# Moving one spill pair and four accumulating transfers among the queues of a hybrid decoder layer

## The chip, the cores and the metric

The kernel runs on one core of a Trainium2 chip. The metric is the time of one execution on the device, in microseconds (us). A core has five engines that run side by side, each through its own list of instructions in order: TensorE (PE, matrix multiplies), VectorE (DVE), ScalarE (ACT), GpSimd (POOL) and SyncE (SP, which here only issues transfers). An engine whose next instruction waits for a semaphore holds up all that stands behind it in its list. Transfers (DMAs) are issued by SP, ACT or POOL and then run on 16 shared DMA engines.

## The reference

The kernel computes one layer of a decoder trunk for 512 positions and a width of 1024. What matters here is its first third:

```python
h = layer_norm(x, ln_emb_g, ln_emb_b)
proj = h @ w_in[i]
(q_att, c_kv, q_idx, k_idx, w_idx, cv_b, cv_c, cv_x, g_att, g_conv) = jnp.split(proj, split_points, axis=-1)
...
score = jnp.einsum('bqhs,bqh->bqs', jax.nn.relu(raw), wb.astype(jnp.float32))
_, sel = lax.top_k(score, topk)
...
conv_y = cv_b * causal_dwconv(cv_c * cv_x, mix_conv_w[i], mix_conv_b[i])
merged = (jax.nn.sigmoid(g_att + b_gate[i, 0]) * (att @ w_br_att[i])
          + jax.nn.sigmoid(g_conv + b_gate[i, 1]) * (conv_y @ w_br_conv[i]))
h = layer_norm(DEEPNORM_ALPHA * h + merged @ w_o[i], ln1_g[i], ln1_b[i])
```

A light indexer scores every earlier key, each query keeps its 128 best keys, and attention runs over those. A short gated convolution runs beside it. Both are gated, summed and projected, and the residual `ALPHA * h` is added. A gated MLP follows, which the change does not touch.

## The kernel before: how the work is staged

**Numbers.** All products are made in a reduced matrix format with a correction: each operand is split into a high and a low part, and three matmuls replace one (L157 to L159: high by high, low activation by high weight or the reverse). The weights come in chunks of 512 KB. A chunk goes through three stages: SP loads it (`wr`, L54), ACT makes the high part (`wh`, L76), and DVE or POOL makes the low part (`wl`, L143, by `Chunk.lo_eng`). Four raw buffers and four pairs of high and low parts rotate, so a load waits until the low part of the chunk four places before has been made.

**Steps.** `plan` writes the program as a list of steps, one chunk of matmuls each, and `run` (L1709) records them in order: first `advance` (loads and splits of chunks that are due), then the `preps` of that step in the order in which they were put there, then the step's own function. Every engine's list comes from this one recording. From step 5 on, `run` also takes some rounds of the top-k selection (`topk`, L588) behind every step. A round is a maximum of 8 and a replacement on DVE (L595, L597), 16 rounds make a block's selection, and a single DVE instruction turns it into a mask `madd` (L600). That is done for three blocks of queries, with 256, 384 and 512 keys.

The steps around the change are 0 to 3 (the indexer's queries `qi`), 4 and 5 (second halves of the first convolution inputs `c` and `x`, each followed by scores), 6 (convolution gate `b`; its number is `at_first`), 7 to 10 (attention queries `qa`), and 11 to 19 (three more triples `c`, `x`, `b` of the convolution). Steps 18 and 20 hold the first attention steps (`att_step`): PE makes logits, DVE and ACT make probabilities `p` (L670 to L678), and PE transposes them (`pT`, L686).

**Row sums.** The later gate products go by blocks (a 2 by 2 scheme in which sums of blocks of rows are multiplied). It needs four sums of the transposed activations `hx`, made in place by accumulating transfers that POOL issues (`first_sum`, L793 to L797). In the names of the order listing:

- sum 0: hx_282 += hx_404
- sum 1: hx_404 += hx_410
- sum 2: hx_410 += hx_282
- sum 3: hx_289 += hx_410

Each sum but the first writes a tile that the sum before it reads, or reads one that it writes, so a sum's issue waits until the sum before has landed. The results are split by `first_parts` at steps 15 to 19 and are first multiplied about 240 us into the run.

**Residual.** The residual `ALPHA * h` is prepared in DRAM. For each of the four blocks of x, DVE scales it by the gain (`res_gain`, L1027), SP spills it (`res_spill`, L1030, tensor `hsp`), and POOL issues a transfer that adds the scaled shift `be` onto it (`res_shift`, L1033). It is read back at about 284 us (`res_rows`). The scales of blocks 2 and 3 stand in `last_rows`, which step 5 calls between its matmuls and its scores (`self.between`, L934).

**Other POOL work there.** POOL also makes low parts of chunks (`wl`), the low part of a small weight (`w_uk`, `w_uv`, L623), the two additions of a convolution (`cvt`, L754), the low part of its result (`cvT`, L773) and of the attention queries (`qa`, L153).

The order is set by these lines of the kernel before:

```python
        for n in range(4):
            self.preps.setdefault((3, 5, 6, 7)[n], []).append(lambda n=n: first_sum(n))
...
        def last_rows():
            res_gain(2)
            res_gain(3)
...
                          (at_first, res_spill, 2), (at_first, res_spill, 3),
                          (at_first + 1, res_shift, 2), (at_first + 1, res_shift, 3), (at_slot[17], res_rows)):
```

Of the kernel before, what the change touches and what calls it, by code (L numbers as in the profile page):

```python
# [85 lines left out]
class Kern:  # L86
# [424 lines left out]
    def plan(self):  # L511
# [281 lines left out]
        def first_sum(n):  # L793

            b11, b12, b21, b22 = (self.hblock[g, h] for g in range(2) for h in range(2))
            to, what = ((b11, b12), (b12, b22), (b22, b11), (b21, b22))[n]
            nc.gpsimd.dma_start(to, what, accum_op=OP.add, max_dma_last_dim=4096)  # L797
# [168 lines left out]
        at_first = len(self.steps)  # L966
# [7 lines left out]
        at_slot, pairs = [], {}  # L974
        for i, o in enumerate(order):
# [24 lines left out]
            n = att_at.get(i)  # L1000
# [6 lines left out]

        self.preps.setdefault(2, []).append(first_flip)
        for n in range(4):
            self.preps.setdefault((3, 5, 6, 7)[n], []).append(lambda n=n: first_sum(n))  # L1010


        self.h1 = []
# [12 lines left out]
        def res_gain(b):  # L1026
            nc.vector.tensor_tensor(self.xb[b], self.xb[b], self.res["ge"], op=OP.mult)  # L1027

        def res_spill(b):
            nc.sync.dma_start(self.hdram[b], self.xb[b])  # L1030
# [16 lines left out]
        def last_rows():  # L1047
            res_gain(2)
            res_gain(3)

        self.between = last_rows
        for at, f, *v in ((1, res_scale, "ge"), (2, res_gain, 0), (2, res_gain, 1), (3, res_spill, 0), (3, res_spill, 1),
                          (1, res_load, "be", "ln_emb_b"), (4, res_scale, "be"), (5, res_shift, 0), (5, res_shift, 1),
                          (at_first, res_spill, 2), (at_first, res_spill, 3),
                          (at_first + 1, res_shift, 2), (at_first + 1, res_shift, 3), (at_slot[17], res_rows)):
            self.preps.setdefault(at, []).append(lambda f=f, v=v: f(*v))

        self.zps = {}
# [429 lines left out]
        n = len(those)  # L1488
# [323 lines left out]
```

## Time and profile before

| What | Value |
|---|---|
| Median of 3 runs | 747.59 us (747.19 to 749.47) |
| The profiled execution's own time | 747.88 us |
| Its span (first to last instruction of the program) | 746.1 us |
| Granted TensorE clock, mean | 0.988 |
| PE busy | 725.3 us (97%) |
| DVE busy | 615.0 us (82%) |
| ACT busy | 427.7 us (57%) |
| POOL busy | 264.5 us (35%) |
| DMA, mean | 244 GB/s |

The profile is one execution. Its views give, for every instruction, a start counted from the span's start, a duration, the idle time of its engine just before it and, in brackets, what ended that idle time. A row of a timeline merges neighbouring instructions of one line ("x2"), and then its duration runs from the first one's start to the last one's end. An instruction's recorded duration holds any time for which it was held up after its start. "SPq" marks an issue of a transfer by SP. POOL's issues of transfers occupy POOL itself.

### The profile page before, as it was taken

To read this page: it belongs to the slowest core of one execution; us is meant where nothing else is said; L and a number is where in the kernel's file an instruction comes from. 1 tells how busy PE (TensorE), PEld (TensorE's weight loads), DVE (VectorE), ACT (ScalarE), POOL (GpSimd) and SP (SyncE) were. 2 spreads that over 40 slices of the span, in tenths; PEclk is the share of its full clock that TensorE was granted. 3 is DMA by queue.
4 is the path that set the end of the run, shared out by engine and by line. 5 is a ranking of instruction groups with operands and counts; after the bars stand their busy time and mean duration, and the time that the engine had idled before them with its cause. 6 is when DMAs were issued, how large, how long until landed. Compare 5 with 4: busy or idle time off the path is not lost.

```text
span 746.1 us, 12222 instructions
## 1 busy us (share of the span) xinstructions
PE 725.3 (97%) x4399; PEld 639.9 (86%) x4399; DVE 615.0 (82%) x1041; ACT 427.7 (57%) x720; POOL 264.5 (35%) x336
## 2 busy tenths in 40 slices
PE   8999997979999999999999999999999999999995
PEld 5998885758887998888888999999999998888885
DVE  5878999977546765679898899999998899978796
ACT  5667322557776654442575666777777665655640
POOL 4315682757665860410101223433332212121002
PEclk9999999989999999999999999999999999999998
DMA  9468896777999999475997999989899869989761
GB/s 354 141 210 236 230 323 228 254 254 182 273 232 185 196 241 353 179 279 201 304 382 260 314 280 253 245 243 249 232 248 243 243 192 224 276 246 251 259 216 56
DMA packets 63019, 182.21 MB, mean 244 GB/s; under 512 B 7360, under 2 KB 7488, under 8 KB 62576
## 3 DMA queue, kind: packets, MB, share of 16 engines
q1 hardware_dynamic: 43968, 140.56, 53.8%
q0 software_dynamic: 18128, 39.46, 29.4%
q10 hardware_dynamic: 864, 1.43, 0.5%
q8 instruction: 34, 0.56, 0.3%
q14 instruction: 25, 0.20, 0.1%
HBM read 171.46 MB, written 72.88 MB: 327 GB/s over the span
## 4 chain that ended last, share of the span: by engine, by line
PE 83%; DVE 12%; DMA 2%; ACT 1%; issue 1%; SPq 0%; DVEq 0%; ACTq 0%
PE ffb L815 26%; PE gtb L815 5%; PE dn L1543 5%; PE dn L1542 5%; PE dn L1544 5%; DVE tk L597 4%; DVE m L595 3%; PE gt L157 2%; PE br L157 2%; PE wo L919 2%; PE wo L920 2%; PE br L159 2%; PE gt L159 2%; PE gt L158 2%; PE br L158 2%; PE wo L918 2%
## 5 line engine op out<-in xcount | busy, mean ns | idle before, releaser
L143 DVE TENSOR_TENSOR wl<-wr,wh 128x1024 fp32r<-128x1024 f32 (+1 forms) x175 | 198.1, 1148 | 42.3 <-ACT wh L76 41.6
L76 ACT CAST wh<-wr 128x1024 fp32r<-128x1024 f32 (+1 forms) x186 | 180.5, 978 | 76.1 <-DMA wr<-in_w_dn 13.5
L1469 POOL TENSOR_TENSOR behind<-token,neghalf 128x1 f32<-128x1 f32 x112 | 79.3, 815 | 242.1 <-ACT token L1468 205.7
L815 PE MATMUL ffb<-hsl,wh 128*128 128x256 f32 x304 | 86.0, 283 | 0.0
L815 PE MATMUL ffb<-hsh,wl 128*128 128x256 f32 x304 | 86.0, 283 | 0.0
L815 PE MATMUL ffb<-hsh,wh 128*128 128x256 f32 x304 | 86.0, 283 | 0.0
L815 PE MATMUL ffb<-h1T,wh 128*128 128x256 f32 x456 | 83.8, 283 | 0.0
L815 PEld LDWEIGHTS ffb<-h1T,wh 128*128 128x128 f32 x456 | 71.2, 192 | 0.1
L815 PE MATMUL ffb<-h1T,wl 128*128 128x256 f32 x228 | 64.7, 284 | 0.1
L815 PEld LDWEIGHTS ffb<-hsl,wh 128*128 128x128 f32 x304 | 58.4, 192 | 0.0
L815 PEld LDWEIGHTS ffb<-hsh,wh 128*128 128x128 f32 x304 | 58.4, 192 | 0.0
L815 PEld LDWEIGHTS ffb<-hsh,wl 128*128 128x128 f32 x304 | 58.4, 192 | 0.0
L143 POOL TENSOR_TENSOR wl<-wr,wh 128x1024 fp32r<-128x1024 f32 x15 | 39.8, 2711 | 18.0 <-ACT wh L76 18.0
L815 PEld LDWEIGHTS ffb<-h1T,wl 128*128 128x128 f32 x228 | 43.7, 192 | 0.4 <-DVE wl L143 0.3
L185 POOL TENSOR_TENSOR rstd<-veps,neghalf 128x1 f32<-128x1 f32 x12 | 8.0, 666 | 98.7 <-DVE nm L208 65.6
L1345 POOL DMA_DIRECT2D ws<-ws x38 | 37.5, 1084 | 13.4 <-issue 8.2
L1345 POOL DMA_DIRECT2D ws<-in_w_a x38 | 36.8, 1369 | 6.1 <-issue 2.7
L157 PE MATMUL cv<-hT,wh 128*128 128x512 f32 x80 | 32.4, 405 | 2.8 <-ACT wh L76 2.4
L159 PE MATMUL cv<-hT,wl 128*128 128x512 f32 x80 | 32.2, 402 | 2.3 <-POOL wl L143 2.3
L158 PE MATMUL cv<-hT,wh 128*128 128x512 f32 x80 | 31.9, 398 | 0.0
L742 DVE SCALAR_TENSOR_TENSOR ff<-c,vec,ff 128x510 f32<-128x510 f32 x38 | 28.5, 750 | 1.3
L739 ACT ACTIVATE ff<-c,vec 128x512 f32<-128x512 f32 x38 | 29.3, 812 | 0.5 <-DVE c L1390 0.5
(364 smaller groups left out, 2089.8 us busy)
## 6 DMA issues: line engine op xcount, KB each, us to landing
wr<-in_w_a SPq DMA_DIRECT2D x61, 512.0 KB, 4.5
ws<-in_w_a SPq DMA_DIRECT2D x76, 256.0 KB, 6.4
wr<-ws SPq DMA_DIRECT2D x38, 512.0 KB, 6.2
ws<-in_w_a POOLq DMA_DIRECT2D x38, 256.0 KB, 8.5
ws<-ws POOLq DMA_DIRECT2D x38, 256.0 KB, 10.9
wr<-in_w_b SPq DMA_DIRECT2D x15, 512.0 KB, 4.9
wr<-in_w_dn SPq DMA_DIRECT2D x15, 512.0 KB, 6.9
wr<-in_w_a SPq DMA_DIRECT2D x19, 256.0 KB, 6.7
```

The costliest lines, as they stand in the source:

```text
L76: nc.scalar.copy(hi, raw)
L143: (self.nc.vector if eng == "v" else self.nc.gpsimd).tensor_tensor(lo, raw, hi.bitcast(F32), op=OP.subtract)
L157: t.matmul(out, wh, xh, start=start, stop=False)
L158: t.matmul(out, wh, xl, start=False, stop=False)
L159: t.matmul(out, wl, xh, start=False, stop=stop)
L597: nc.vector.match_replace(nxt, m8, cur, PICKED)
L815: nc.tensor.matmul(o, l[:, c], r, start=start and c + i == 0, stop=stop and c == 3 and i == 2, skip_group_check=True)
L1345: return lambda: nc.gpsimd.dma_start(to, what, accum_op=OP.add, max_dma_last_dim=4096)
L1469: nc.gpsimd.tensor_tensor(self.sm("behind", [P, 1], bufs=2), t, self.neghalf, op=OP.mult)
L1542: nc.tensor.matmul(o, ah, wh[:, i, c], start=first, stop=False, skip_group_check=free)
L1543: nc.tensor.matmul(o, ah, wl[:, i, c], start=False, stop=False, skip_group_check=free)
L1544: nc.tensor.matmul(o, al, wh[:, i, c], start=False, stop=last, skip_group_check=free)
```

## The change

Three edits, none of which adds or removes an instruction:

1. Row sums 0 to 3 are issued at steps 3, 4, 5, 6 and no longer at 3, 5, 6, 7.
2. The spills of blocks 2 and 3 stand in `last_rows`, behind the two scales, and no longer at step 6.
3. The shifts of blocks 2 and 3 are issued at step 6, behind row sum 3, and no longer at step 7.

```diff
         for n in range(4):
-            self.preps.setdefault((3, 5, 6, 7)[n], []).append(lambda n=n: first_sum(n))
+            self.preps.setdefault(3 + n, []).append(lambda n=n: first_sum(n))
...
         def last_rows():
             res_gain(2)
             res_gain(3)
+            res_spill(2)
+            res_spill(3)
...
-                          (at_first, res_spill, 2), (at_first, res_spill, 3),
-                          (at_first + 1, res_shift, 2), (at_first + 1, res_shift, 3), (at_slot[17], res_rows)):
+                          (at_first, res_shift, 2), (at_first, res_shift, 3),
+                          (at_slot[17], res_rows)):
```

What this makes of the engines' lists is seen in two places. The first is POOL's list from row sum 1 on. `hx` rows are row sums, `hsp` rows are shifts (180 to 183 are blocks 0 to 3), and the numbers behind the names tell tiles apart. Before:

```order
L797 DMA hx_404<-hx_410 128x1024
L1033 DMA hsp_180<-be 128x1024
L1033 DMA hsp_181<-be 128x1024
L623 TENSOR_TENSOR w_uk<-w_uk_raw,w_uk 128x512
L754 TENSOR_TENSOR cvt_956<-cvt_956,tap_958 128x511
L754 TENSOR_TENSOR cvt_956<-cvt_956,tap_961 128x510
L143 TENSOR_TENSOR wl_1023<-wr_608,wh_1022 128x1024
L797 DMA hx_410<-hx_282 128x1024
L773 TENSOR_TENSOR cvT_1062<-cvy_1060,cvT_1062 128x512
L143 TENSOR_TENSOR wl_1078<-wr_766,wh_1077 128x1024
L797 DMA hx_289<-hx_410 128x1024
L1033 DMA hsp_182<-be 128x1024
```

The same stretch of POOL's list with the change:

```order
L797 DMA hx_404<-hx_410 128x1024
L797 DMA hx_410<-hx_282 128x1024
L1033 DMA hsp_180<-be 128x1024
L1033 DMA hsp_181<-be 128x1024
L623 TENSOR_TENSOR w_uk<-w_uk_raw,w_uk 128x512
L754 TENSOR_TENSOR cvt_957<-cvt_957,tap_959 128x511
L754 TENSOR_TENSOR cvt_957<-cvt_957,tap_962 128x510
L143 TENSOR_TENSOR wl_1026<-wr_608,wh_1025 128x1024
L797 DMA hx_289<-hx_410 128x1024
L1033 DMA hsp_182<-be 128x1024
L1033 DMA hsp_183<-be 128x1024
L773 TENSOR_TENSOR cvT_1065<-cvy_1063,cvT_1065 128x512
```

Row sum 2 now stands right behind row sum 1, ahead of the shifts of blocks 0 and 1 and of `w_uk`. Row sum 3 and the shifts of blocks 2 and 3 now stand ahead of `cvT` and the low part behind it, and no longer behind them. What follows on POOL (`qa`, `wl`, `w_uv` and so on) keeps its order.

The second place is SP's list, from the third chunk load before the spills on. `wr` rows are chunk loads, `hsp` rows are spills, and the first `ws` row begins a series of copies of weights for a later stage. Before:

```order
L54 DMA wr_845<-in_w_a 128x1024
L54 DMA wr_920<-in_w_a 128x1024
L54 DMA wr_1026<-in_w_a 128x1024
L1030 DMA hsp_182<-x_73 128x1024
L1030 DMA hsp_183<-x_74 128x1024
L1333 DMA ws_116<-in_w_a 128x512
```

And with the change:

```order
L54 DMA wr_845<-in_w_a 128x1024
L54 DMA wr_921<-in_w_a 128x1024
L1030 DMA hsp_182<-x_73 128x1024
L1030 DMA hsp_183<-x_74 128x1024
L54 DMA wr_1029<-in_w_a 128x1024
L1335 DMA ws_116<-in_w_a 128x512
```

The two spills have passed one chunk load (its tile is called wr_1026 before and wr_1029 after). PE, DVE and ACT execute the same instructions in the same order as before.

## The prediction

> **What bounds the kernel now.** I read the page first, then PE's idle times, then the chain of work that ended last, and then the timelines of POOL and DVE in the stretch that the change touches. The shares of that chain by engine, from the page:
>
> ```profile
> PE 83%; DVE 12%; DMA 2%; ACT 1%; issue 1%; SPq 0%; DVEq 0%; ACTq 0%
> ```
>
> PE is the bound but not all of it: 12% of the chain is DVE. So the question is where PE stands still for DVE. The timeline of PE, its rows with idle time between 90 and 170 us (start, duration, instruction, in brackets the idle time before it and what ended it):
>
> ```profile
> 94.96 0.50 PE L159 MATMUL cv<-hT,wl 128*128 128x512 f32 x1 [0.21 <-POOL wl L143]
> 127.16 0.79 PE L157 MATMUL cv<-hT,wh 128*128 128x512 f32 x1 [2.43 <-ACT wh L76]
> 130.44 0.80 PE L159 MATMUL cv<-hT,wl 128*128 128x512 f32 x1 [2.06 <-POOL wl L143]
> 147.31 0.50 PE L157 MATMUL cv<-hT,wh 128*128 128x512 f32 x1 [0.37 <-DVE cvy L770]
> 162.11 0.45 PE L686 MATMUL pT<-ident,p 128*128 128x128 f32 x1 [3.62 <-DVE p L678]
> 164.99 0.45 PE L686 MATMUL pT<-ident,p 128*128 128x128 f32 x1 [1.79 <-DVE p L678]
> ```
>
> These six sum to 10.48 us, and they are what any speed-up of the other engines here can give back. The last two wait for DVE's probabilities. The chain of work that ended last shows what made DVE late:
>
> ```profile
> 95.92 13.52 DVE madd L600
> ...
> 161.67 3.18 DVE p L678 x5
> ```
>
> One DVE instruction, the mask of the first selection, lasts from 95.92 to 109.44. The waits at 127.16 and 130.44 hang on it too: ACT and POOL, in their order, stood behind a convolution input that DVE made only after it. POOL's timeline over the same time:
>
> ```profile
> 84.94 1.29 POOL L773 TENSOR_TENSOR cvT<-cvy,cvT 128x512 fp32r<-128x512 f32 x1 [6.64 <-ACT cvT L772]
> 86.19 2.40 POOL L143 TENSOR_TENSOR wl<-wr,wh 128x1024 fp32r<-128x1024 f32 x1
> 88.54 0.89 POOL L797 DMA_DIRECT2D hx<-hx  x1
> 89.13 2.10 POOL L1033 DMA_DIRECT2D hsp<-be  x2
> 90.25 2.30 POOL L153 TENSOR_TENSOR qa<-qac,qa 128x512 fp32r<-128x512 f32 x1
> 91.51 3.40 POOL L143 TENSOR_TENSOR wl<-wr,wh 128x1024 fp32r<-128x1024 f32 x1
> ...
> 102.33 2.25 POOL L153 TENSOR_TENSOR qa<-qac,qa 128x512 fp32r<-128x512 f32 x1
> 103.58 5.70 POOL L143 TENSOR_TENSOR wl<-wr,wh 128x1024 fp32r<-128x1024 f32 x2
> ```
>
> POOL runs without a pause from 84.94 to 109.28, and the mask ends 0.16 us later. I read this as DVE kept out of something that POOL holds. Ahead of the three issues a POOL instruction starts when the one before it ends (86.19 against 84.94 + 1.29 = 86.23). Behind them it starts 1 us early: `qa` at 90.25 while the second shift's issue runs to 91.23, `wl` at 91.51 while `qa` is recorded to 92.55. From the issues on POOL always has its next instruction begun, and there is no seam for DVE.
>
> Where POOL runs without that overlap, DVE does get in at a seam. A later mask on DVE's timeline, and POOL's:
>
> ```profile
> 130.73 1.11 DVE L600 TENSOR_SCALAR madd<-tk 128x384 f32<-128x384 f32 x1
> ```
>
> ```profile
> 130.34 1.29 POOL L773 TENSOR_TENSOR cvT<-cvy,cvT 128x512 fp32r<-128x512 f32 x1
> 131.58 2.51 POOL L143 TENSOR_TENSOR wl<-wr,wh 128x1024 fp32r<-128x1024 f32 x1
> ```
>
> This mask ended at 131.84, 0.21 us after `cvT` (130.34 + 1.29 = 131.63), with POOL's next instruction standing right behind. The same at 170 us, DVE and then POOL:
>
> ```profile
> 169.31 2.12 DVE L143 TENSOR_TENSOR wl<-wr,wh 128x1024 fp32r<-128x1024 f32 x1
> ```
>
> ```profile
> 167.62 2.71 POOL L754 TENSOR_TENSOR cvt<-cvt,tap 128x511 f32<-128x511 f32 x2 [2.87 <-ACT tap L753]
> 170.30 3.40 POOL L143 TENSOR_TENSOR fsl<-hx,fsh 128x1024 fp32r<-128x1024 f32 x1
> ```
>
> DVE ended 1.09 us after the pair at 170.33, and POOL's next lasted 3.40 where a free one takes 2.40 (86.19 row).
>
> **The change part by part.** Row sum 2 moves ahead of the shifts of blocks 0 and 1 and of `w_uk`. POOL's timeline there now, and the time from issue to landing of the four row sums:
>
> ```profile
> 62.07 0.88 POOL L797 DMA_DIRECT2D hx<-hx  x1
> 62.67 2.06 POOL L1033 DMA_DIRECT2D hsp<-be  x2
> 69.99 1.91 POOL L623 TENSOR_TENSOR w_uk<-w_uk_raw,w_uk 128x512 fp32r<-128x512 f32 x1 [5.25 <-ACT w_uk L622]
> 71.88 2.78 POOL L754 TENSOR_TENSOR cvt<-cvt,tap 128x511 f32<-128x511 f32 x2
> 75.08 2.38 POOL L143 TENSOR_TENSOR wl<-wr,wh 128x1024 fp32r<-128x1024 f32 x1 [0.42 <-ACT wh L76]
> 77.40 0.89 POOL L797 DMA_DIRECT2D hx<-hx  x1
> ```
>
> ```profile
> DMA to landing us min/median/max: 5.9/7.0/7.7
> ```
>
> Row sum 2 waits at the head of POOL's list for row sum 1 (62.07) to land: at 69.1 by the median, 68.0 to 69.8 by the ends. Three issues take 2.66 us (62.07 to 64.73), so POOL is free at 71.7. Then `w_uk` at 1.29 (the size of `cvT`) and the pair at 2.78 end at 75.8, and `wl` starts 0.7 us later than 75.08. With another tenth for DVE's scores, which take turns with these three, I take 0.8 (0 to 1.5 by the landings; a gain is excluded, since `wl` waits for ACT until 75.08). Queued behind the waiting issue are just these; POOL idles there today until 69.99.
>
> DVE's scores and the first rounds move along by 0.8, and with them `cvy`, on which `cvT` waits by way of ACT (the 84.94 row). DVE's timeline:
>
> ```profile
> 72.31 7.28 DVE L585 SCALAR_TENSOR_TENSOR score<-rl,widx,score 128x512 f32<-128x512 f32 x6 [1.56 <-ACT rl L583]
> ...
> 83.51 0.68 DVE L770 TENSOR_TENSOR cvy<-cv,cvt 128x512 f32<-128x512 f32 x1
> ```
>
> So POOL's long run starts at 85.74. Row sum 3 and the shifts of blocks 2 and 3 leave that run: they took it from 88.59 to 91.23, 2.64 us. They now go into the pause between 78.3 and 85.7, if nothing holds them. Row sum 3 waits for row sum 2 (issued at 69.1, landed by 76.8 at the latest row). The shifts wait for the spills. DVE's scales, SP's issues, and the landing of the two spills now:
>
> ```profile
> 68.39 2.35 DVE L1027 TENSOR_TENSOR x<-x,ge 128x1024 f32<-128x1024 f32 x2
> ```
>
> ```profile
> 62.14 15.68 SPq L54 DMA_DIRECT2D wr<-in_w_a  x3
> 77.91 1.13 SPq L1030 DMA_DIRECT2D hsp<-x  x2
> ```
>
> ```profile
> DMA to landing us min/median/max: 7.5/8.1/8.7
> ```
>
> SP issues the spills at 77.91 because they stand behind a chunk load that waits for a raw buffer. In front of it they go at the scales' end, the second at 70.74, and land at 79.4 by today's 8.7. The traffic beside them is heavier (row sum 2 and two shifts), so I allow up to 83. The last issue then ends between 80.9 and 84, ahead of 85.74. The load that they pass goes out when POOL's `wl` is done, as before, and costs nothing.
>
> Now the run: `cvT` 85.74, `wl` to 89.4, `qa` to 90.7, `wl` to 93.1, `w_uv` to 94.4, `qa` to 95.7, `wl` to 98.0 (1.29 and 2.38 each). The mask comes at 96.7 and enters at the seam at 98.0; with the 0.21 us of the later mask it ends at 98.25, 11.2 us earlier than 109.44.
>
> [...]
>
> What is late next? With 11.2 us, `p` is there at 150.9 while PE, rid of 0.21, 2.43, 2.06, 0.37 and 3.62, comes for it at 153.4. The second batch (164.99) would be there at 153.8, PE at 154.5. POOL's `wl` for the 130.44 wait is done 11 us earlier as well. So all 10.48 us go. Against it, the 0.8 us of lateness can show as a wait for the next `wl`, as at 94.96: between 0 and 0.8, I take 0.3, the size of that row. The sum is -10.48 + 0.3 = -10.2 us.
>
> The profiled execution took 747.88 us (span 746.1, so 1.8 lie around it), 0.3 above the median of 747.59. 747.88 - 10.2 = **737.7 us**. Less would go where a shifted DVE instruction meets another POOL one, 2.4 us each at most, of which PE's slack of 2.5 us hides the most; so 736.5 to 741 for this case.
>
> **The rivals.** *The run stays closed.* The overlap could come from the chain of ready POOL instructions itself and not from the issues ahead of it. Then the mask ends when the run does: 109.44 - 2.64 + 0.8 = 107.6, 1.8 us earlier, and PE gains that: 746.0. A hole could open ahead of the last `wl`, whose high part waits for a load:
>
> ```profile
> 104.90 1.05 ACT L76 CAST wh<-wr 128x1024 fp32r<-128x1024 f32 x1 [3.97 <-DMA wr<-in_w_a]
> ```
>
> That gives 105.95 against a POOL that is there at 105.4 (98.0 and two `qa` and two `wl` more); the mask would enter then and end at 105.6, a gain of 3.8: 744.1. For this rival: 13.52 us is the only row of its length. Against it: two seams did let DVE in. I take 745, the middle.
>
> *The spills land late (slower).* POOL sits on the last shift, and `cvT` with the whole run behind it. The run without issues lasts 109.28 - 84.94 - 2.64 = 21.7 us, the last issue about 1 us. A landing after 84 puts the issues in front of the run again and the mask waits through; it ends as late as now for a landing at 86.7, and each us after that costs one. The spill at 70.74 would have to take 16 us, against 8.7 in the row. At twice that row, 88.1, the time is 749.3, and the `wl` that PE then needs is late as well: 749 to 751. [...]
>
> *Nothing changes.* A landing between 84 and 86.7, or a mask that gains and then loses it to other POOL instructions: 746 to 748.
>
> **How the numbers follow.** Main case 0.66, closed run 0.18, late spills 0.08, nothing 0.08. About 0.3% (2.2 us, so below 745.3) is what a measurement of this kernel can tell. The main case is faster, and the closed run half of it: 0.66 + 0.09 = 0.75. Same: 0.09 + 0.08 = 0.17. Slower: 0.08. The range takes the main case from 736.3 and the closed run to 746.2, and leaves out the other two and some edges.
>
> **What would show it.** Right: the first mask lasts about 1.5 us or less; POOL's row sum 3 and two shifts lie before 85 us; PE's waits at 127, 130 and 162 are gone. Wrong: the first mask still ends with POOL's run, or `cvT` on POOL waits behind a shift, or PE's waits return elsewhere by 170 us.

## The result, and the profile after

The changed kernel took 736.57 us (median; 735.2 to 737.32), the kernel before, run beside it, 748.4 us (747.19 to 749.47). The ratio is 0.984, with a 95% interval of 0.9816 to 0.9864: 1.6% faster. The forecast was 737.7 us, in a range of 736.3 to 746.2. The profiled execution took 735.2 us with a span of 733.4, against 747.88 and 746.1 before: 12.7 us less. The ratios in this document leave out executions in a slower state of the chip, one of them here: 746.65 us, of the kernel with the spills' part alone.

The chain's shares by engine, from the page of the kernel after:

```profile
PE 81%; DVE 13%; DMA 3%; issue 1%; ACT 1%; SPq 0%; DVEq 0%; ACTq 0%
```

They hardly differ from before (83% and 12%). The shares of a chain do not show a stall of 13 us in 746; the waits do. PE's timeline of the kernel after, the same stretch as before, all rows with an idle time of 0.2 us or more and the first gate matmul behind them:

```profile
89.89 0.50 PE L159 MATMUL qa<-hT,wl 128*128 128x512 f32 x1 [0.52 <-POOL wl L143]
...
153.28 0.82 PE L686 MATMUL pT<-ident,p 128*128 128x128 f32 x4 [1.53 <-DVE p L678]
...
155.66 0.50 PE L157 MATMUL gt<-hT,wh 128*128 128x512 f32 x1
```

The waits at 94.96, 127, 130, 147 and 162 are gone. The last of the six is left, at 153.28, and one at 89.89 is new: 2.05 us together. The first gate matmul of the kernel before, on the same view:

```profile
168.50 0.50 PE L157 MATMUL gt<-hT,wh 128*128 128x512 f32 x1
```

From 168.50 to 155.66 is 12.84 us, so the whole gain is made by this point. DVE's timeline of the kernel after, the first mask and one of the eight scalings of the probabilities:

```profile
97.16 0.46 DVE L600 TENSOR_SCALAR madd<-tk 128x256 f32<-128x256 f32 x1
...
150.75 2.39 DVE L678 TENSOR_SCALAR p<-p,rs 128x128 f32<-128x128 f32 x1
```

The mask lasts 0.46 us instead of 13.52 and ends at 97.62, 11.8 us earlier. The scaling comes beside a `wl` of POOL's (150.71, 2.35 us) and ends 0.08 us after it; the first scalings take 0.28 us each. That is not new, as the same scaling of the kernel before shows:

```profile
162.46 2.38 DVE L678 TENSOR_SCALAR p<-p,rs 128x128 f32<-128x128 f32 x1
```

POOL's timeline of the kernel after:

```profile
69.21 0.85 POOL L797 DMA_DIRECT2D hx<-hx  x1 [6.19 <-DMA hx<-hx]
...
78.67 0.89 POOL L797 DMA_DIRECT2D hx<-hx  x1
79.26 1.19 POOL L1033 DMA_DIRECT2D hsp<-be  x1
80.95 0.86 POOL L1033 DMA_DIRECT2D hsp<-be  x1 [0.50 <-issue]
86.18 1.30 POOL L773 TENSOR_TENSOR cvT<-cvy,cvT 128x512 fp32r<-128x512 f32 x1 [4.37 <-ACT cvT L772]
...
91.06 2.39 POOL L143 TENSOR_TENSOR wl<-wr,wh 128x1024 fp32r<-128x1024 f32 x1
94.91 1.30 POOL L623 TENSOR_TENSOR w_uv<-w_uv_raw,w_uv 128x512 fp32r<-128x512 f32 x1 [1.47 <-ACT w_uv L622]
96.17 1.29 POOL L153 TENSOR_TENSOR qa<-qac,qa 128x512 fp32r<-128x512 f32 x1
97.43 2.46 POOL L143 TENSOR_TENSOR wl<-wr,wh 128x1024 fp32r<-128x1024 f32 x1
```

The transfers are out of the run, as predicted. The mask (97.16 to 97.62) got in at the seam between `qa` and `wl` (97.43 to 97.46). But there is a row that the prediction did not have: POOL now **pauses** for 1.47 us ahead of `w_uv`. ScalarE's timeline of the kernel after says why, the load's issue and the high part that waits for it:

```profile
85.75 0.34 ACTq L620 DMA_DIRECT2D w_uv_raw<-in_w_uv  x1
...
94.21 0.62 ACT L622 CAST w_uv<-w_uv_raw 128x512 fp32r<-128x512 f32 x1 [5.25 <-DMA w_uv_raw<-in_w_uv]
```

The same two rows of the kernel before:

```profile
84.50 0.33 ACTq L620 DMA_DIRECT2D w_uv_raw<-in_w_uv  x1
...
90.54 0.62 ACT L622 CAST w_uv<-w_uv_raw 128x512 fp32r<-128x512 f32 x1 [2.83 <-DMA w_uv_raw<-in_w_uv]
```

Before, the load came 6.0 us after its issue, and POOL, kept busy by three transfers to issue, came for it later. Now it takes 8.4 us, and POOL is there first. The shifts' transfers, issued at 79.26 and 80.95, run beside it: the load took 6.4 us in the kernel with the row sums alone (below), whose shifts are issued behind it, and 8.2 in the one with the spills and shifts alone. So two things changed at once ahead of the mask: no transfer is issued in the run, and the run has a pause in it. The experiments have to tell which one lets DVE in.

### The profile page after: what moved, and what is told of

It reads as the page before. It is cut to its first block, busy times and chain, and to the rows that moved or that the text cites. A ratio compares the mean times of both kernels' runs of the same rounds, so it can differ in the third digit from the quotient of the medians.

```text
span 733.4 us, 12223 instructions
## 1 busy us (share of the span) xinstructions
PE 721.4 (98%) x4399; PEld 638.0 (87%) x4399; DVE 604.3 (82%) x1041; ACT 427.3 (58%) x720; POOL 268.4 (37%) x336
## 4 chain that ended last, share of the span: by engine, by line
PE 81%; DVE 13%; DMA 3%; issue 1%; ACT 1%; SPq 0%; DVEq 0%; ACTq 0%
PE ffb L815 22%; PE gtb L815 5%; PE dn L1546 5%; PE dn L1545 5%; PE dn L1544 5%; DVE tk L597 4%; DVE m L595 3%; PE gt L157 2%; PE br L157 2%; PE gt L159 2%; PE wo L919 2%; PE wo L920 2%; PE br L158 2%; PE gt L158 2%; PE br L159 2%; PE wo L918 2%
## 5 line engine op out<-in xcount | busy, mean ns | idle before, releaser
L1471 POOL TENSOR_TENSOR behind<-token,neghalf 128x1 f32<-128x1 f32 x112 | 85.3, 871 | 239.0 <-ACT token L1470 204.3
L1347 POOL DMA_DIRECT2D ws<-ws x38 | 39.9, 1200 | 11.4 <-issue 6.1
L143 POOL TENSOR_TENSOR wl<-wr,wh 128x1024 fp32r<-128x1024 f32 x15 | 36.3, 2421 | 17.7 <-ACT wh L76 17.7
L157 PE MATMUL cv<-hT,wh 128*128 128x512 f32 x80 | 31.4, 392 | 0.0
L158 PE MATMUL cv<-hT,wh 128*128 128x512 f32 x80 | 31.1, 389 | 0.0
L1273 ACT ACTIVATE ff<-ff 128x512 f32<-128x512 f32 x22 | 13.8, 633 | 27.2 <-DVE ff L742 27.2
```

Of the source, the lines that this page charges most:

```text
L143: (self.nc.vector if eng == "v" else self.nc.gpsimd).tensor_tensor(lo, raw, hi.bitcast(F32), op=OP.subtract)
L157: t.matmul(out, wh, xh, start=start, stop=False)
L158: t.matmul(out, wh, xl, start=False, stop=False)
L1347: return lambda: nc.gpsimd.dma_start(to, what, accum_op=OP.add, max_dma_last_dim=4096)
L1471: nc.gpsimd.tensor_tensor(self.sm("behind", [P, 1], bufs=2), t, self.neghalf, op=OP.mult)
```

## The experiments

Kernels that are set side by side ran on the same chip with the kernel before, four at a time in the order of the table (medians of the kernel before 749.32, 748.51 and 749.65 us). The "seam theory" in the expectations of the first group is the prediction's: transfers make POOL's records overlap, which leaves no seam. Theory A is the form that the first group left of it: a transfer that POOL issues at the head of an unbroken run keeps DVE out until POOL next pauses. Theory B arose from the first group: no transfer matters as such, and DVE gets in only where POOL's next instruction has become ready late. Theory C is on PE's clock.

| kernel | first mask us | median us | ratio to before, 95% interval |
|---|---|---|---|
| after + one POOL transfer behind `w_uv` | 13.01 | 750.04 | 0.9989 to 1.0016 |
| after + two of them | 13.63 | 752.81 | 1.0026 to 1.0056 |
| before, masks with an accumulator | 0.42 | 733.02 | 0.9767 to 0.9797 |
| row sums alone | 12.60 | 750.59 | 1.0008 to 1.0041 |
| after + a POOL subtraction behind `w_uv` | 1.11 | 738.17 | 0.9836 to 0.9887 |
| after, `w_uv`'s load earlier | 0.73 | 737.13 | 0.9827 to 0.9892 |
| before, two mask instructions with accumulators | 0.42 | 736.20 | 0.9812 to 0.9863 |
| before + PE kept busy in its waits | 13.51 | 747.12 | 0.9964 to 0.9996 |
| after + POOL transfer ahead of `w_uv` | 0.56 | 735.64 | 0.9779 to 0.9857 |
| after + the transfer from ScalarE | 1.42 | 736.99 | 0.9796 to 0.9876 |
| spills and shifts alone | 0.30 | 734.73 | 0.9748 to 0.9860 |
| after, masks and p with accumulators | 0.42 | 739.01 | 0.9818 to 0.9894 |

### One transfer put back

```diff
+        junk = [self.dram.tile([P, R], F32, name=f"junk{i}", tag=f"junk{i}") for i in range(1)]
+        for t in junk:
+            self.preps[8].append(lambda t=t: nc.gpsimd.dma_start(t, self.kvg))
```

> The changed kernel with one small extra transfer (64 KB, from a loaded constant to a scratch tensor that nobody reads) issued by POOL between w_uv and the second qa, in the middle of the run in which the first mask comes. Seam theory (an issue of a transfer right ahead of ready POOL instructions makes them overlap, and DVE finds no seam until POOL stands still): the first mask, 0.46 us in the changed kernel, lasts 11 to 13 us and ends when the run does, at about 110; the time goes back to 746 to 749. It is open whether one issue, which is 0.3 us longer than the time to the next start, is enough. Rival (the mask came free because transfers moved out of this time, or because of POOL's pause at 93.4 to 94.9): both are still so, the issue costs its own 0.9 us on POOL, the mask lasts at most 3 us, 736 to 738.

Measured: 750.04 us (748.52 to 750.82), as slow as the kernel before. One transfer of 64 KB that nobody waits for gives the whole 13 us back. DVE's timeline, then POOL's:

```profile
97.17 13.01 DVE L600 TENSOR_SCALAR madd<-tk 128x256 f32<-128x256 f32 x1
```

```profile
94.96 1.29 POOL L623 TENSOR_TENSOR w_uv<-w_uv_raw,w_uv 128x512 fp32r<-128x512 f32 x1 [1.52 <-ACT w_uv L622]
96.19 0.61 POOL L1684 DMA_DIRECT2D junk<-kvg  x1
96.82 1.31 POOL L153 TENSOR_TENSOR qa<-qac,qa 128x512 fp32r<-128x512 f32 x1
98.07 2.42 POOL L143 TENSOR_TENSOR wl<-wr,wh 128x1024 fp32r<-128x1024 f32 x1
...
105.30 4.73 POOL L143 TENSOR_TENSOR wl<-wr,wh 128x1024 fp32r<-128x1024 f32 x2
```

Everything up to 96 us is as in the kernel after, DVE comes to the mask at the same moment, and it ends with POOL's run again (110.18 against 110.03). One sign of the prediction falls: behind the transfer `wl` starts at 98.07, only 0.06 us ahead of the end of `qa` (96.82 + 1.31 = 98.13), so the 1 us overlap of POOL's records is not needed for the run to be closed. The transfer itself is over long before; the DMA view of this kernel, its last column the median time from issue to landing:

```profile
junk<-kvg POOLq DMA_DIRECT2D x1, 64.0 KB, 5.0
```

Issued at 96.19, it had landed by about 101.2, and DVE stayed out for 9 us more.

### Two transfers put back

The same line with `range(2)`.

> The same with two such small transfers in a row. Seam theory: the overlap is 0.6 us or more, the mask waits for the end of the run, 747 to 750. Rival: 1.8 us on POOL, 736 to 739. If the kernel with one issue is fast and this one slow, the overlap has to reach a size before it closes the seams.

Measured: 752.81 us and a mask of 13.63 us. The second transfer adds its own length to the run (0.55 us) and closes nothing more. The median is 2.8 us above that with one transfer, and the profile, of the fastest of the five executions (750.38 us), does not show where the rest comes from.

### The mask in a form that does not wait

```diff
-            nc.vector.tensor_scalar(self.madd[b], cur, LIMIT, DROP, op0=OP.is_ge, op1=OP.mult)
+            nc.vector.tensor_scalar(self.madd[b], cur, LIMIT, DROP, op0=OP.is_ge, op1=OP.mult,
+                                    accum_out=self.sm("mark", [P, 1], bufs=2))
```

> The kernel before, whose only change is that the three mask instructions also write out an accumulated value that nobody reads. All transfers and issues stand where they stood. Seam theory (the mask waits for something that POOL's instructions hold, and this form does not need it): the first mask lasts under 1 us although POOL runs overlapped from 90 to 109 as before, and the time falls by most of what the change gave: 735 to 739. Rival (the time came from where the transfers stand): nothing moves, 746 to 749. If this form needs the same thing, 746 to 749 too, with a mask of 13 us; then only the profile tells.

Written so, the kernel does not compute the layer (relative error 0.87): I take it to leave out the mask's multiplication by `DROP` (-1e30), so that the other keys stay in, and only its time counts. Measured: 733.02 us (732.49 to 733.71), the fastest of all. DVE's timeline, then POOL's:

```profile
95.87 0.42 DVE L600 TENSOR_SCALAR_CACHE_REDUCE madd<-tk 128x256 f32<-128x256 f32 x1
```

```profile
93.83 2.27 POOL L624 TENSOR_TENSOR w_uv<-w_uv_raw,w_uv 128x512 fp32r<-128x512 f32 x1
95.09 2.27 POOL L153 TENSOR_TENSOR qa<-qac,qa 128x512 fp32r<-128x512 f32 x1
```

This is the kernel before with its transfers in the run, POOL's closed run is just where it was (`w_uv` at 93.83 against 93.88, `qa` at 95.09 against 95.11), and the mask takes 0.42 us in the middle of it. So the 13.52 us were a wait beside POOL's run that this form (0.42 us) does not have, and the gain hangs on the masks alone; the other two, which have the new form as well, had lasted 1.11 and 0.43 us.

### Row sums alone

```diff
-            self.preps.setdefault((3, 5, 6, 7)[n], []).append(lambda n=n: first_sum(n))
+            self.preps.setdefault(3 + n, []).append(lambda n=n: first_sum(n))
```

> The first edit alone: row sums at steps 3 to 6, spills and shifts where they were. Two issues (the shifts of blocks 2 and 3) still stand in front of the run. Seam theory: the overlap stays, the mask lasts over 10 us, 746 to 749 (the run is 0.6 us shorter by one issue and starts 1.2 us later), unless POOL pauses for w_uv before the mask comes, which would open the seams. Rival (the row sums' place is what counts): 736 to 740.

Measured: 750.59 us, ratio 1.0008 to 1.0041, so if anything slower than before. DVE's timeline, then POOL's:

```profile
97.30 12.60 DVE L600 TENSOR_SCALAR madd<-tk 128x256 f32<-128x256 f32 x1
```

```profile
89.91 1.75 POOL L1033 DMA_DIRECT2D hsp<-be  x2
...
94.69 1.91 POOL L623 TENSOR_TENSOR w_uv<-w_uv_raw,w_uv 128x512 fp32r<-128x512 f32 x1
95.95 1.90 POOL L153 TENSOR_TENSOR qa<-qac,qa 128x512 fp32r<-128x512 f32 x1
```

Two shifts still stand in the run, POOL has no idle time behind them, and the run is closed. The records overlap by 0.65 us here (94.69 + 1.91 = 96.60 against 95.95), by 1 us before and by 0.06 us in the run above, with a mask of 12.6 to 13.5 us in all three.

### A subtraction in place of the transfer

```diff
+        fill = self.small.tile([P, 256], F32, name="fill", tag="fill", bufs=1)
+        done = self.small.tile([P, 256], F32, name="done", tag="done", bufs=1)
+        nc.gpsimd.memset(fill, 0.0)
+        self.preps[8].append(lambda: nc.gpsimd.tensor_tensor(done, fill, fill, op=OP.subtract))
```

> The kernel after, with one more subtraction on POOL (256 elements of a scratch tile, about 0.65 us by half of cvT's 1.30) put between w_uv's low part and the second qa, where the first of the junk transfers stood; no transfer is added. Theory A (a transfer issued ahead of POOL's run is what shuts VectorE out): nothing is issued there, so the first mask gets in at an early seam, under 3 us, and the time is that of the kernel after plus at most 0.6, 736 to 738. Theory B (VectorE gets in only at a seam where POOL's next instruction had become ready late, under about a us before the running one ended): POOL is 0.65 us later, ScalarE's high part for the next wl is ready 1.3 us before the seam, the seam stays shut as with the junk transfer: first mask 12 to 13.5 us, time 748 to 751.

Measured: 738.17 us, a mask of 1.11 us. DVE's timeline, then POOL's:

```profile
97.28 1.11 DVE L600 TENSOR_SCALAR madd<-tk 128x256 f32<-128x256 f32 x1
```

```profile
96.37 0.61 POOL L1685 TENSOR_TENSOR done<-fill 128x256 f32<-128x256 f32 x1
96.94 1.30 POOL L153 TENSOR_TENSOR qa<-qac,qa 128x512 fp32r<-128x512 f32 x1
98.20 2.47 POOL L143 TENSOR_TENSOR wl<-wr,wh 128x1024 fp32r<-128x1024 f32 x1
```

The subtraction takes 0.61 us in the place where the transfer took 0.61 us, POOL's next instructions come within 0.13 us of where they came there, and the mask gets in at the seam at 98.20. Theory B falls: POOL's order and lateness are the same in both kernels, and only the kind of the instruction differs. ScalarE's high part for the `wl` at the seam was ready 1.33 us ahead of it there and 1.28 us here. This pair is the cleanest of the study.

### The load of w_uv one step earlier

```diff
+        def latent_load(name):
+            self.latent_w[name] = self.k2(f"{name}_raw")
+            nc.scalar.dma_start(self.latent_w[name], a[name])
...
+        self.preps.setdefault(7, []).insert(0, lambda: latent_load("w_uv"))
```

> The kernel after, with w_uv's load issued one step earlier, so that ScalarE and POOL do not pause for it at 93.45 to 94.91 us. No transfer of POOL's is added. Theory A (transfers issued ahead of the run): the first mask gets in as in the kernel after, under 3 us, time 735 to 737. Theory B (seams are open only where POOL's next instruction becomes ready late): without the pause ScalarE is far ahead again, so the mask stays out for the whole run, 11 to 13 us, time 747 to 750.

Measured: 737.13 us (736.15 to 741.39), mask 0.73 us. This run tells the theories apart less than it was meant to. ScalarE's timeline:

```profile
85.82 0.34 ACTq L619 DMA_DIRECT2D w_uv_raw<-in_w_uv  x1
...
94.70 0.62 ACT L627 CAST w_uv<-w_uv_raw 128x512 fp32r<-128x512 f32 x1 [5.53 <-DMA w_uv_raw<-in_w_uv]
```

ScalarE stood behind `cvT`'s high part until 85.68 either way, so the load left at 85.82 instead of 85.75 and the pause stayed. A step earlier in a list is not earlier in time where the queue waits.

### The transfer ahead of the pause

```diff
+        junk = self.dram.tile([P, R], F32, name="junk", tag="junk")
+        self.preps.setdefault(8, []).append(lambda: nc.gpsimd.dma_start(junk, self.kvg))
         for n, name in ((5, "w_uk"), (8, "w_uv")):
```

> The kernel after with the one 64 KB junk transfer of the earlier run, now issued by POOL ahead of w_uv instead of behind it, so that POOL's pause for w_uv (93.45 to 94.91 us) lies between the issue and the run of subtractions. Theory A (an issue at the head of an unbroken run of POOL shuts VectorE out until POOL next pauses): the pause comes after the issue, the mask gets in within 2.5 us, time 736 to 739. Rival (a POOL transfer in flight or just issued shuts VectorE out whatever POOL does in between): first mask 11 to 13.5 us, time 748 to 751.

Measured: 735.64 us, mask 0.56 us. DVE's timeline, then POOL's:

```profile
97.03 0.56 DVE L600 TENSOR_SCALAR madd<-tk 128x256 f32<-128x256 f32 x1
```

```profile
93.24 0.61 POOL L1681 DMA_DIRECT2D junk<-kvg  x1
94.89 1.28 POOL L623 TENSOR_TENSOR w_uv<-w_uv_raw,w_uv 128x512 fp32r<-128x512 f32 x1 [1.04 <-ACT w_uv L622]
```

The same transfer, one place earlier in POOL's list: with the pause of 1.04 us behind it, it costs nothing that can be measured (735.64 us, a mask of 0.56); in front of `qa`, without a pause behind it, it costs 13 us (750.04, a mask of 13.01). It was still under way when the mask came (by its 5.0 us to landing, until 98.2), so a transfer in flight did not keep DVE out here either.

The kernel after holds a second case of this, ahead of `cvT`. Row sum 2 and two shifts (69.21 to 71.86) stand there right in front of POOL's `w_uk` and the pair of `cvt`, and DVE comes to a score while `w_uk` runs. DVE's timeline of the kernel before:

```profile
72.31 1.40 DVE L585 SCALAR_TENSOR_TENSOR score<-rl,widx,score 128x512 f32<-128x512 f32 x1 [1.56 <-ACT rl L583]
```

And of the kernel after:

```profile
72.42 2.55 DVE L585 SCALAR_TENSOR_TENSOR score<-rl,widx,score 128x512 f32<-128x512 f32 x1 [1.61 <-ACT rl L583]
```

With the issues in front, the score stays out at the end of `w_uk` (70.86 + 2.31 = 73.17) and ends 0.56 us after the first `cvt` (72.12 + 2.29 = 74.41), behind which POOL pauses until 74.48. In the kernel with the row sums alone POOL's `w_uk` and pair of `cvt` last as long as here (2.32 and 3.82 us against 2.31 and 3.80). So a pause of 0.07 us was enough there, and the change makes a short closed run of its own.

### The transfer from ScalarE

```diff
+        junk = self.dram.tile([P, R], F32, name="junk", tag="junk")
+        self.preps[8].append(lambda: nc.scalar.dma_start(junk, self.kvg))
```

> The kernel after with the same 64 KB junk transfer, issued by ScalarE right behind w_uv's high part instead of by POOL, within about a us of the same moment. If it is POOL's issuing that shuts VectorE out, the mask gets in within 2.5 us and the time is 736 to 739 (ScalarE loses about 0.4 us to the issue). If it is the traffic of the transfer, first mask 11 to 13.5 us, time 748 to 751.

Measured: 736.99 us, mask 1.42 us. It falls on the side of POOL's issuing, but ScalarE, which issued the transfer first (95.61), made its high part of `qa` late, and POOL paused for 0.86 us right ahead of the mask, so that by Theory A it would have been open in either case. It adds little.

### Spills and shifts alone

The rest of the change without the row sums' new steps: `first_sum` stays at steps 3, 5, 6 and 7.

> The other parts of the change alone: spills beside their scale and shifts 2 and 3 one step earlier, row sums left where they were in the kernel before, so that one issue of a row sum stays behind wl21 at the head of POOL's run. Theory A: one issue is enough, first mask 12 to 13.5 us, time 747 to 751, ratio 0.998 to 1.003. Rival (it is the number of issues, and fewer let VectorE in): mask under 5 us, time 737 to 742.

Measured: 734.73 us, ratio 0.9748 to 0.9860. Neither expectation held: by Theory A's number the run should have been closed, and by the rival's the time should have been above 737. DVE's timeline, then POOL's:

```profile
95.83 0.30 DVE L600 TENSOR_SCALAR madd<-tk 128x256 f32<-128x256 f32 x1
```

```profile
88.46 0.86 POOL L797 DMA_DIRECT2D hx<-hx  x1
89.08 1.56 POOL L153 TENSOR_TENSOR qa<-qac,qa 128x512 fp32r<-128x512 f32 x1
90.33 2.66 POOL L143 TENSOR_TENSOR wl<-wr,wh 128x1024 fp32r<-128x1024 f32 x1
93.43 1.29 POOL L623 TENSOR_TENSOR w_uv<-w_uv_raw,w_uv 128x512 fp32r<-128x512 f32 x1 [0.44 <-ACT w_uv L622]
```

A row sum is issued in the run, and POOL's records overlap behind it (89.08 + 1.56 = 90.64 against 90.33). But without the two shifts POOL comes to `w_uv` earlier, `w_uv`'s load lands later than before, and a pause of 0.44 us opens. Behind it the records no longer overlap, and the mask gets in at once. The number expected leaves such a pause out; by the two runs with the transfer on either side of the pause (13.01 and 0.56 us), the run had to be open. So this part of the change makes the whole gain by itself, and `cvT` is not late here (84.85, against 86.18 in the kernel after). The row sums' part alone gives nothing, and beside the other it costs that 1.3 us of POOL's time.

The pause is a thin thing to rest on: one of this kernel's four executions took 746.65 us with a mean granted clock of 0.990, where the kernel before shows 0.987 to 0.992 and the other three 0.996 to 0.998. No profile shows what it did; that the pause failed to open in it is only a guess.

### PE kept busy in its waits

PE's granted clock had no place in the prediction. The windows of the kernel before around two of its waits (from and to, busy time of PE, PEld, DVE, ACT and POOL, and the granted clock, DMA share and rate):

```profile
127.00:131.00 4.00, 1.78 (x3) 1.00 (x4) 3.83 (x11) 1.50 (x3) 4.00 (x3) 0.50 0.00 0
...
165.00:168.00 3.00, 3.00 (x22) 2.64 (x24) 2.93 (x8) 1.88 (x3) 0.38 (x1) 0.50 0.54 175
```

PE's granted clock is 0.50 in two stretches of 6.83 us, 127.02 to 133.85 and 161.16 to 167.98, each starting in a wait, and 1.00 in the kernel after (60 to 728 us). PE's busy time fell by about 4 us with that (725.3 to 721.4), and I took it for a term of 4 us that the prediction had left out.

```diff
+                o = self.ps("cv")
+                if (kind, j) == ("b", 2):
+                    hold(o, 18)
...
                 t = self.ps("pT")
+                if b == 0:
+                    hold(t, (27, 14)[g])
```

`hold` writes so many transposes of the identity into a PSUM tile that the next matmuls overwrite.

> The kernel before, with idle transposes on TensorE in its waits at 125, 158 and 163 us (18, 27 and 14 of 128x128, about 1.9, 2.9 and 1.5 us at full clock), into PSUM tiles that the next matmuls overwrite; the mask still waits 12 to 14 us. Theory C (the two stretches of 6.83 us at half clock cost about 4 us that the prediction left out): the granted clock stays at 1.0 and the time is 3 to 4.5 us below the kernel before, ratio 0.994 to 0.996. Rival: TensorE would wait for the same instructions of POOL, VectorE and ScalarE anyway, so the clock is worth under 1 us, ratio 0.999 to 1.002.

Measured: 747.12 us against 748.51, ratio 0.9964 to 0.9996: 1.4 us, between the two. The clock fell in one stretch of 3.41 us instead of two of 6.83 (mean clock 0.86 from 127 to 131 us, 0.81 from 131 to 137). The same kind of window of this kernel, at full clock:

```profile
165.00:168.00 3.00, 3.00 (x31) 2.48 (x32) 2.93 (x8) 1.87 (x3) 0.36 (x1) 1.00 0.46 175
```

PE's timeline of this kernel, the second batch of `pT` and the first gate matmul:

```profile
164.90 0.92 PE L692 MATMUL pT<-ident,p 128*128 128x128 f32 x4 [0.45 <-DVE p L678]
...
167.37 0.50 PE L157 MATMUL gt<-hT,wh 128*128 128x512 f32 x1
```

The second batch starts at 164.90, as before (164.99): until then PE waits for DVE, and the faster clock did not bring it forward by more than 0.09 us. Only what follows the last wait is shorter, by 168.50 - 167.37 = 1.13 us. So with the mask still late the clock is a real term, but of 1.1 us and not of 4.

### A mask that computes the same, and one step further

```diff
+            nc.vector.tensor_scalar(self.madd[b], cur, LIMIT, None, op0=OP.is_ge, op1=OP.max,
+                                    accum_out=self.sm("mark", [P, 1], bufs=2))
+            nc.vector.tensor_scalar(self.madd[b], self.madd[b], DROP, None, op0=OP.mult, op1=OP.max,
+                                    accum_out=self.sm("mark", [P, 1], bufs=2))
```

> The kernel before, its three mask instructions each written as two that keep an accumulator (the comparison, then the multiplication by the constant), which computes the same mask. If the form with an accumulator never waits for POOL, as the single one with the accumulator showed (0.42 us, 733.02): both under 1 us each, time 732.5 to 734.5, ratio 0.977 to 0.981 to the kernel before, and below the kernel after. If that one ran freely for another reason: first mask 13 us, time 748 to 751.

In the kernel before: 736.20 us. Both instructions take 0.42 us beside POOL, without any of the change under study. It equals the change, and misses the 732.5 to 734.5 expected. Each mask costs DVE one instruction more here, and PE waits 1.27 us for DVE at 161.72, as it does in the next kernel (1.25 us at 161.06).

> The kernel after with its masks as two instructions with an accumulator each, and the scaling of p (L678) with an accumulator too, so that neither waits for POOL; it computes the same. The wait of 1.53 us for p at 151.8 us goes, if the accumulator form runs beside POOL there as the mask's did; a mask costs one instruction more: 733 to 736, ratio to the kernel before 0.978 to 0.983. If p waits on something else, the time stays at 736 to 737.

With the change and with `p` in this form as well: 739.01 us, the slowest of the kernels whose mask got in early. DVE's timeline, one of the eight scalings of `p` and the low part behind the next masks:

```profile
151.25 0.34 DVE L681 TENSOR_SCALAR_CACHE_REDUCE p<-p,rs 128x128 f32<-128x128 f32 x1
...
157.03 3.29 DVE L143 TENSOR_TENSOR wl<-wr,wh 128x1024 fp32r<-128x1024 f32 x1
```

PE's timeline of the same kernel, its rows with idle time from 155 to 192 us:

```profile
161.06 0.47 PE L157 MATMUL gt<-hT,wh 128*128 128x512 f32 x1 [1.25 <-DVE token L1472]
190.38 1.52 PE L166 MATMUL lg<-kT,qa 64*128 64x512 f32 x5 [1.56 <-DVE sig L908]
```

`p` no longer waits beside POOL's `wl`, and the wait of 1.53 us at 153.28 is gone. DVE's own `wl`, which has no accumulator, meets POOL's `fsl` (156.84, 2.40 us) and takes 3.29 us, against 1.22 beside POOL's 128x1 instructions at 257.13 in the kernel before. Waits of 1.25 and 1.56 us take the place of the one removed. No version here that computes the same is measurably better than the kernel with the spills' part alone.

## Why the prediction was right, point by point

- **The time** lies only 0.27 us inside the range (736.57 against 736.3, or 736.5 in another sentence of the prediction), and the profiled execution, 735.2, lies below it: the sum was -10.2 us and the span fell by 12.7. The mechanism came out in the main; that the number stayed in the range is partly luck.
- **POOL's and SP's places** came out: row sum 2 at 69.21 (69.1 predicted), the last shift's issue over at 81.8 (80.9 to 84), the spills at 69.70 as soon as the scales were done. The late spills of the slower rival did not come: `cvT` waited for ScalarE and not for a shift.
- **The lateness of `cvT`** was taken at 0.8 us and was 86.18 - 84.94 = 1.24, inside the bounds of 0 to 1.5. On PE it showed as 0.52 us (0.3 taken). Its way was another than "scores, which take turns with these three": 1.15 us of it is the score that the three issues ahead of `w_uk` kept out (2.55 us instead of 1.40).
- **The mask** was forecast to enter at a seam and to end at 98.25; it ended at 97.62. It was the seam behind `qa` and not the one behind `wl`, since the pause had moved POOL's run, so it is luck that the two times are this close. What held it before was named rightly: a transfer of POOL's in front of an unbroken run, shown by one transfer against one subtraction in the same place (13.01 against 1.11 us). The sign that I read it from, records that overlap by 1 us, was no condition (0.06 us in the closed run with the added transfer).
- **The step that failed is "Now the run: `cvT` 85.74, `wl` to 89.4 ... `w_uv` to 94.4"**: I let POOL run through without a pause, because `w_uv` was ready in time before. Its load took 8.4 us instead of 6.0, and the pause that this made opens the run by itself: the spills' part alone keeps a transfer in the run and is as fast. What the change needs is fewer issues ahead of `w_uv`, not none.
- **"These six sum to 10.48 us, and they are what any speed-up of the other engines here can give back"** was too low, and "So all 10.48 us go" too high. PE's waits fell by 10.48 - 2.05 = 8.43 us. The other 4.41 of the 12.84 us are PE's own work: of the 13.65 us at half clock, some 8.7 were work and the rest waits, and none of it runs at half clock after. Matmuls of 128x512 start 0.43 us apart there (131.03 to 133.16) and 0.23 us apart at full clock (134.18 to 136.90), so at full clock that work takes some 4.1 us less, an estimate from these rows. Seen from DVE, the second batch of `pT` moved by 164.99 - 153.28 = 11.71 us, as the end of the mask did (11.82), and the way from there to the gate matmul shrank by 1.13 us at full clock. Kept up alone, the clock gives only the 1.1 us, because the second batch then still starts at 164.90.
- **What is late next**: the sum had PE come for the second batch at 154.5, with "PE's slack of 2.5 us" in front of DVE. At full clock PE came at 151.75, and 1.53 of the 1.79 us stayed. The scaling of `p` that meets POOL's `wl` there was no new collision (2.38 us before, 2.39 after).
- **The closed run** (0.18, priced at 745): as a state of POOL it is real. With a transfer in front it took 750 and not the 746.0 of a run without a hole. The mask ended at 110.18 instead of 107.6, since POOL's run began 0.46 us later and the pause of 1.52 us and the transfer's 0.61 us were not in the price; that is 2.6 of the 4 us. The mask lasted 12.6 to 13.6 us, across seven or eight of POOL's instructions, in five kernels, and 1.11 us, to the next seam, in the kernel with the subtraction.

Not settled is what in POOL a transfer changes, so that later seams stay shut until a pause. A run with neither a transfer nor a pause ahead of the mask was not had, since the earlier load did not take the pause away.

## What to carry to other kernels

When one engine's instruction lasts many times its usual length beside a busy POOL, change its form first (here an accumulator: 0.42 us for 13.5), and only then the order of what is around it. Look for the last point at which POOL was idle: here a POOL transfer behind it shut a plain tensor_scalar out of a whole run of large subtractions (13.01 us), and one ahead of it did not (0.56). This was seen with large POOL instructions alone: from 245.62 to 262.99 us of the kernel before, POOL's records show no idle time between fourteen transfers and its 128x1 instructions, and DVE's `wl` took 1.22 us there, as when free. Price a removed wait by how far the work that ends last moves (12.84 us here), not by the idle time on the waiting engine (8.43), whose clock may have been lowered (0.50 here).

## What the runs showed of the hardware

- With one POOL transfer of 64 KB, 0.61 us to issue, at the head of POOL's run, a DVE tensor_scalar that took 0.30 us at its shortest lasted 13.01 us, across seven POOL instructions (`qa` at 96.82 to the last `wl`) and 9 us beyond the transfer's landing. With a pause of 1.04 us behind the transfer it lasted 0.56 us, with one of 0.44 us behind a row sum 0.30; for a score, a pause of 0.07 us was enough.
- In the kernel before, PE's granted clock fell to 0.50 for 6.83 us each in PE waits of 2.43 and 3.62 us. With PE kept busy it fell for 3.41 us, beside a wait of 2.56 us, and in the kernel after, with a wait of 1.53 us, it did not fall from 60 to 728 us. The mean granted clock was 0.988 in the kernel before, 0.995 with PE kept busy and 0.997 after. What length of wait lowers the clock, or whether the length alone does, was not shown.
- A tensor_scalar with an accumulator took 0.42 us where the plain one lasted 13.52, on the same data beside the same POOL run.
